# A hybrid decoder layer on one core: the sparse experts' second table summed on TensorE in four column strips, and token groups of 256, 384 and 384

## The chip, the core and the metric

One core of a Trainium2 chip runs the whole program; the other seven cores rest. The metric is the time of one execution on the device in microseconds (us), lower being better. The program was timed in three runs, and one further execution was profiled, from which all rows come.

## What is computed

One layer of a decoder, for 1024 prompt tokens of width 1024 and for 8 sample tokens with states of their own, all in float32. Three mixers read one combined input projection (88 blocks of 128 columns): a state-space scan (SSD), a convolution with 31 taps, and attention over 256 memory tokens. Their outputs are gated, merged, projected and normalised. Then each token picks 8 x 16 of 16,384 experts, and each expert is a row `u` of one table and a row `v` of another:

```python
def _peer_block(t, w_q, sub_keys, u_tab, v_tab):
    qv = (t @ w_q).reshape(nt, PEER_HEADS, 2, PEER_DHALF)
    s = jnp.einsum('thkd,hknd->thkn', qv, sub_keys)
    s_top, i_top = lax.top_k(s, PEER_TOPK)
    ...
    best, pos = lax.top_k(cand.reshape(nt, PEER_HEADS, PEER_TOPK * PEER_TOPK), PEER_TOPK)
    idx = jnp.take_along_axis(...)
    gate = jax.nn.softmax(best.astype(jnp.float32), axis=-1).astype(t.dtype)
    u = jnp.take(u_tab, idx, axis=0)
    act = jax.nn.gelu(jnp.einsum('td,thkd->thk', t, u), approximate=False)
    v = jnp.take(v_tab, idx, axis=0)
    return jnp.einsum('thk,thkd->td', gate * act, v)
```

The scan works in chunks of 128 tokens. Per chunk and head it needs the decays `exp(a_cs[l] - a_cs[s])` for l >= s, with `a_cs` a running sum over the chunk.

## The kernel before

**Groups.** The prompt passes in four groups (GROUPS 128, 128, 384, 384). For each, `front` loads the transposed tokens and computes the time steps (L465), and `main` runs the mixers over the group's input products (`proj`), its output products (`out_product`) and `merge`. A weight block is 128 x 1024. In the groups of 128 (PLAIN) a product is 8 matmuls in float32 (`product`, L197), each of which leaves two records. In the groups of 384, `load_w` splits a weight block in two fp32r parts (ScalarE L175, VectorE L177) and `mm3` multiplies three pairs of parts, 24 matmuls of one record each (L186). The output products are float32 matmuls (L197) everywhere. A product's result lies in one of three PSUM banks named mm. In `merge` a bank with an output product waits while another holds the product for its gate. The samples' columns ride with group 1 (RIDE).

**Decays.** For four heads of a chunk, `ssd_group` fills a bank with four mask matmuls in bf16 (L804) and four float32 matmuls that spread the running sums (L805), and ScalarE takes four exponentials.

**Routing.** When the next group begins, `routing` of the one before runs in small steps among its matmuls (`tick`): query products, top 16 on VectorE, and `route`. The last group's routing has no later group to run in.

**Sparse experts.** For the 640 tokens of the first three groups, `peer_block` and `peer_experts` treat 128 tokens at a time. For each of 128 slots GpSimd gathers 128 rows of the first table, one a token, into a buffer uv of 128 x 1024 (L404; five buffers), and VectorE multiplies each row by its token and sums it (L413). Then for each slot 128 rows of the second table are gathered, and VectorE adds them, scaled, to pacc (L423). The step of one slot is a row. `spread` puts rows between the products, PACE and PHASES rows a product; they are issued only after the fourth last of VectorE's other instructions (`issue_after` of `behind`), and at the lowest priority.

**Dense experts.** The last group's 384 tokens take all 16,384 experts (`dense_group`). First a table of gates is made in four steps: one-hot rows on VectorE (L1160), scalings on ScalarE (L1164), matmuls (L1165), and ScalarE's evictions (L1169). Meanwhile 30 of 128 blocks of activations (`x u`, L186 into the banks tp and sp) are computed and kept in memory. Then a loop over the 128 blocks loads and splits `v` (512 columns at a time), weighs the activations by the gates, and adds the second product into six banks (L1226). Rows of the sparse experts are spread through the loop, and what is left runs behind it.

The samples' attention (L990) already multiplies in strips: its four heads write 8 rows each at rows 0, 32, 64 and 96 of one bank, with stationary tiles of 8 columns.

A scheduler orders the instructions of each engine by priority and dependencies; each engine then works through its own queue in order. The numbers of lines below are those of the kernel before; a row of the changed kernel has the numbers of that kernel.

## Time and profile before

| what | us |
|---|---|
| median of three runs | 4664.98 |
| fastest and slowest run | 4653.48, 4665.51 |
| the profiled execution | 4662.57 |
| its span on the core | 4660.8 |
| TensorE matmuls busy | 4028.7 (86%) |
| VectorE busy | 3651.9 (78%) |
| GpSimd busy | 1822.1 (39%) |
| ScalarE busy | 1798.8 (39%) |

The DMA queues moved 1278.27 MB, 274 GB/s over the span. Busy time is the time in which an engine executes; the share is of the span. PE is TensorE's matmuls, PEld its weight loads (which overlap matmuls), DVE VectorE, ACT ScalarE, POOL GpSimd, SP the queue that issues plain transfers. The granted clock (PEclk) is a share of TensorE's full 2.4 GHz.

### The profile page before, as it was taken

What the parts mean: (1) busy time and instruction counts of PE and PEld (TensorE: products, weight loads), DVE (VectorE), ACT (ScalarE), POOL (GpSimd) and SP (SyncE); (2) the same over time, 40 slices, a digit from 0 to 9 for tenths busy, and PEclk for the clock granted to TensorE, in tenths of its full rate; (3) what the DMA queues carried; (4) which work ended last, traced back from release to release, by engine and by line L of the source; (5) the groups of instructions that cost most, each with busy time, mean ns of one, the idle gap of its engine ahead of it and who ended that gap; (6) DMA issues with size and microseconds to landing.
All of it is one profiled execution on the core that took longest, in us unless ns stands there. A gap on an engine that the chain in (4) does not pass through costs nothing.

```text
span 4660.8 us, 61736 instructions
## 1 busy us (share of the span) xinstructions
PE 4028.7 (86%) x20471; PEld 3289.6 (71%) x20471; DVE 3651.9 (78%) x7677; ACT 1798.8 (39%) x4112; POOL 1822.1 (39%) x1614
## 2 busy tenths in 40 slices
PE   9999966899878898899379898879887999789997
PEld 8999866787766665667267686645555788678886
DVE  1363478687888788778987899889785898788898
ACT  3434422274553312344136242022885333323334
POOL 0000034434424325534144544643012465556564
PEclk9999878898889999889688999999998999899999
DMA  6677678877657788867266976987568999899998
GB/s 198 208 238 232 202 296 315 339 247 275 207 184 275 278 286 317 317 227 244 106 236 225 325 249 231 371 279 265 182 218 290 341 387 368 250 356 354 364 386 304
DMA packets 436928, 1278.27 MB, mean 274 GB/s; under 512 B 45264, under 2 KB 119632, under 8 KB 434432
## 3 DMA queue, kind: packets, MB, share of 16 engines
q0 software_dynamic: 186880, 679.56, 41.2%
q1 hardware_dynamic: 249728, 594.77, 36.9%
q8 instruction: 161, 2.64, 0.2%
q14 instruction: 159, 1.30, 0.1%
HBM read 1220.22 MB, written 53.93 MB: 273 GB/s over the span
## 4 chain that ended last, share of the span: by engine, by line
issue 18%; DMA 15%; DVE 12%; PE 11%; POOL 8%; ACT 5%; POOLq 0%; SPq 0%; DVEq 0%; ACTq 0%
POOL uv L404 8%; DMA uv<-in_peer_v,idx 8%; DMA uv<-in_peer_u,idx 3%; PE mm L186 3%; DVE uv L413 2%; DVE pacc L423 2%; PE mm L197 2%; ACT xt L1169 2%; DVE b L535 2%; ACT e L1164 2%; DVE wl L177 1%; PE sp L186 1%; PE mm L1226 1%; DMA e<-in_peer_v 1%; DMA wr<-in_win 1%
## 5 line engine op out<-in xcount | busy, mean ns | idle before, releaser
L404 POOL DMA_INDIRECT uv<-in_peer_u,idx x640 | 800.9, 1251 | 1151.4 <-DVE uv L413 825.9
L404 POOL DMA_INDIRECT uv<-in_peer_v,idx x640 | 832.2, 1300 | 916.5 <-DVE pacc L423 571.9
L413 DVE SCALAR_TENSOR_TENSOR uv<-uv,x 128x1024 f32<-128x1024 f32 (+1 forms) x656 | 789.2, 1220 | 191.2 <-DMA uv<-in_peer_u,idx 173.5
L423 DVE SCALAR_TENSOR_TENSOR pacc<-uv,av,pacc 128x1024 f32<-128x1024 f32 (+1 forms) x650 | 833.0, 1282 | 103.7 <-DMA uv<-in_peer_v,idx 90.2
L186 PE MATMUL mm<-xt,wh 128*128 128x384 f32 x2816 | 793.2, 362 | 30.1 <-ACT wh L175 15.1
L197 PE MATMUL mm<-b,wr 128*128 128x128 f32 (+2 forms) x3072 | 747.8, 398 | 38.1 <-ACT b L648 14.4
L197 PEld LDWEIGHTS mm<-b,wr 128*128 128x128 f32 x3072 | 492.5, 201 | 241.0 <-issue 22.7
L175 ACT ACTIVATE wh<-wr 128x1024 fp32r<-128x1024 f32 x274 | 290.3, 1060 | 866.3 <-DMA wr<-in_win 330.9
L186 PEld LDWEIGHTS mm<-xt,wh 128*128 128x128 f32 x2816 | 541.0, 200 | 67.7 <-ACT wh L175 19.6
L186 PE MATMUL mm<-xt,wl 128*128 128x384 f32 x1408 | 505.3, 360 | 44.5 <-DVE wl L177 44.3
L535 DVE SCALAR_TENSOR_TENSOR b<-raw,cc,b 128x128 f32<-128x128 f32 (+1 forms) x960 | 444.6, 479 | 11.7 <-ACT b L533 4.7
L197 PE MATMUL mm<-xt,wr 128*128 128x128 f32 (+1 forms) x2816 | 368.5, 290 | 18.8 <-DMA wr<-in_win 8.9
L197 PEld LDWEIGHTS mm<-xt,wr 128*128 128x128 f32 x2816 | 354.3, 202 | 28.3 <-issue 11.9
L177 DVE TENSOR_TENSOR wl<-wr,wh 128x1024 fp32r<-128x1024 f32 x274 | 333.8, 1219 | 47.1 <-ACT wh L175 47.0
L186 PEld LDWEIGHTS mm<-xt,wl 128*128 128x128 f32 x1408 | 281.6, 200 | 61.1 <-DVE wl L177 53.5
L1226 PE MATMUL mm<-wh,b 128*128 128x512 f32 x768 | 246.4, 402 | 16.6 <-ACT b L150 16.6
L150 ACT ACTIVATE b<-acc 128x384 fp32r<-128x384 f32 x128 | 66.8, 525 | 377.0 <-PE st L1226 205.1
L186 PE MATMUL tp<-b,wh 128*128 128x384 f32 x784 | 206.9, 346 | 0.0
L186 PE MATMUL sp<-b,wh 128*128 128x384 f32 x784 | 203.5, 341 | 0.5 <-ACT b L682 0.5
L1165 PEld LDWEIGHTS mm<-e,e 128*128 128x128 f32 x768 | 119.4, 208 | 93.9 <-ACT e L1164 82.1
L1226 PE MATMUL ss<-wh,b 128*128 128x512 f32 x512 | 183.7, 399 | 0.0
L753 POOL COPY halo<-raw 128x3 f32<-128x3 f32 x96 | 51.0, 532 | 323.8 <-ACT raw L751 323.1
(392 smaller groups left out, 6951.3 us busy)
## 6 DMA issues: line engine op xcount, KB each, us to landing
wr<-in_win SPq DMA_DIRECT2D x352, 512.0 KB
wr<-in_peer_ut SPq DMA_DIRECT2D x128, 512.0 KB
e<-in_peer_v SPq DMA_DIRECT2D x256, 256.0 KB
wr<-in_wso SPq DMA_DIRECT2D x64, 512.0 KB
wr<-in_wq SPq DMA_DIRECT2D x64, 512.0 KB
gd<-xt SPq DMA_DIRECT2D x16, 1536.0 KB
xt<-gd SPq DMA_DIRECT2D x16, 1536.0 KB
wr<-in_wmo SPq DMA_DIRECT2D x32, 512.0 KB
```

Of the source, the lines that this page charges most:

```text
L175: act.activation(wh, wr, AF.Copy)
L177: dve.tensor_tensor(wl, wr, f32(wh), op=OP.subtract)
L186: pe.matmul(ps, a[:, k], b[k0 + k], start=(i == 0), stop=(i == n - 1))
L197: pe.matmul(ps, w[:, k], xs[k], start=(k == 0), stop=(k == 7))
L404: pool.indirect_dma_start(out=dst, out_offset=None, in_=table, in_offset=bass.IndirectOffsetOnAxis(ap=idx_col, axis=0))
L413: dve.scalar_tensor_tensor(u, u, 1.0, x1, op0=OP.mult, op1=OP.mult, accum_out=av[:, s:s + 1])
L423: dve.scalar_tensor_tensor(acc, v, av[:, s:s + 1], acc, op0=OP.mult, op1=OP.add)
L535: dve.scalar_tensor_tensor(cv, raw[:, i:i + nt], col(C_FW, j * TAPS + i), cv, op0=OP.mult, op1=OP.add)
L1164: act.activation(oj[:, u], oj[:, u], AF.Copy, scale=tr[:, 2, t + u:t + u + 1])
L1165: pe.matmul(pg[:, u * P:(u + 1) * P], oj[:, u], oi[:, u], start=True, stop=True)
L1169: act.activation(gs[:, :, o:o + TG].rearrange("p i t -> p t i"), pg.rearrange("p (t i) -> p t i", t=TG), AF.Copy)
L1226: pe.matmul(outs[2 * tbk + dh], a[:, ts], v[:, dh * 512:dh * 512 + 512], start=(c == 0 and i == 0), stop=(c == P - 1 and i == 2))
```

## The change

**Groups of 256, 384 and 384.** All products of input columns are split (no PLAIN group); the samples ride with group 0. A group's routing still runs in the next one.

**Sparse for 768 tokens, dense for 256.** The first 128 tokens of the last group become a sparse block too (SP); the dense part keeps the last 256 (DN), with 38 blocks of activations ahead of the loop instead of 30 (EARLY), and four banks for its sums instead of six.

**The second table on TensorE.** `block_u` works as before on the first table. It then transposes weights and indices, so that `block_v` can gather the 128 rows of one token into one buffer (a slot a partition). `four` multiplies it with a stationary tile of 32 columns of which one holds the token's weights, in two halves of 512 columns, into strip j (32 partitions) of the banks va. Token 32 j + m goes to strip j, so four tokens make a set. `four` is emitted VLAG, three rows, after the set's last gather. Streams for first table, second table and samples take turns (`row`).

**Decays.** The running sums are cut into three bf16 parts (cs3), and for four heads there is one mask matmul and one of 512 columns for the subtracted term, then four of 128 that add, and a single exponential over 512 columns.

**The rest.** Two mm banks instead of three, and sp becomes the bank st, which makes room for two va banks; eight uv buffers instead of five; halo copies on ScalarE instead of GpSimd; the sum of squares of the scan's output is collected in SBUF; a smaller area for DMA descriptors (4096).

```diff
-GROUPS = (128, 128, 384, 384)
+GROUPS = (256, 384, 384)
...
-QT = 24
+QT = 16
+SP = P
+DN = N - SP
...
-UVB = 5
-PLAIN = (0, 1)
-TICKS = (8, 5, 2, 3)
...
+UVB = 8
...
-PACE = (1.0, 2.0, 5.25)
...
+PACE = (3.0, 1.2, 2.4)
...
-RIDE = 1
+RIDE = 0
...
-EARLY = 30
-STEP = 4
+EARLY = 38
+STEP = 2
+VLAG = 3
+TLAG = 8
...
-        return psp.tile([P, 512], F32, name="mm", bufs=3)
+        return psp.tile([P, 512], F32, name="mm", bufs=2)
...
+    psm = pst
+    def pva():
+        return psp.tile([P, 512], F32, name="va", bufs=2)
...
+    slide = [cst.tile([P, 4, 63], F32, name=f"slide{i}") for i in range(2)]
+    for w in slide:
+        dve.memset(w, 0.0)
...
+    def row():
+        for _ in range(3):
+            i = turn[0] = (turn[0] + 1) % 3
+            queue, start = ((blocks, block_u), (weighed, block_v), (extra, iter))[i]
+            if streams[i] is None and queue:
+                streams[i] = start(queue.popleft())
+            if streams[i] is not None:
+                try:
+                    next(streams[i])
+                    return
+                except StopIteration:
+                    streams[i] = None
...
+            for x in late:
+                x[0] -= 1
+            while late and late[0][0] <= 0:
+                with tc.issue_after(lastpe):
+                    late.popleft()[1]()
             n = len(nc.cur_bb.bb.instructions)
             with tc.issue_after(last), tc.high_priority(-LATER):
-                try:
-                    next(experts[0])
-                except StopIteration:
-                    experts.popleft()
+                row()
...
+    def block_u(b):
+        g, c, idx, gate = b
+        x1 = pep.tile([P, D], F32, name="x1", bufs=1)
+        sp.dma_start(x1, x1d[g][c])
+        av = pep.tile([P, P], F32, name="av", bufs=2)
+        for s in range(P):
+            u = pep.tile([P, D], F32, name="uv", bufs=UVB)
+            gather(u, I["peer_u"], idx[:, c, s:s + 1])
+            dve.scalar_tensor_tensor(u, u, 1.0, x1, op0=OP.mult, op1=OP.mult, accum_out=av[:, s:s + 1])
+            yield
+        act.activation(av, av, AF.Gelu)
+        dve.tensor_tensor(av, av, gate[:, c], op=OP.mult)
+        def turned():
+            ix = blk(P)
+            act.activation(ix, idx[:, c], AF.Copy)
+            pt = pst()
+            pe.transpose(pt[:, 0:P], av, ident)
+            pe.transpose(pt[:, P:2 * P], ix, ident)
+            avt = pep.tile([P, P], F32, name="avt", bufs=2)
+            act.activation(avt, pt[:, 0:P], AF.Copy)
+            ixt = pep.tile([P, P], I32, name="ixt", bufs=2)
+            dve.tensor_copy(ixt, pt[:, P:2 * P])
+            weighed.append((g, c, avt, ixt))
+        late.append([TLAG, turned])
+    def block_v(b):
+        g, c, avt, ixt = b
+        va = []
+        def four(m, vs):
+            if m == 0:
+                va.extend(pva() for _ in range(2))
+            w = slide[m % 2]
+            act.activation(w[:, :, 31], avt[:, m:P:32], AF.Copy)
+            for dh in range(2):
+                for j in range(4):
+                    pe.matmul(va[dh][32 * j:32 * j + 32], w[:, j, 31 - m:63 - m], vs[j][:, dh * 512:dh * 512 + 512],
+                              start=(m == 0), stop=(m == 31))
+        for m in range(32):
+            vs = []
+            for j in range(4):
+                v = pep.tile([P, D], F32, name="uv", bufs=UVB)
+                gather(v, I["peer_v"], ixt[:, 32 * j + m:32 * j + m + 1])
+                vs.append(v)
+                if j < 3:
+                    yield
+            late.append([VLAG, lambda m=m, vs=vs: four(m, vs)])
+            yield
+        done = []
+        late.append([VLAG, lambda: done.append(1)])
+        while not done:
+            yield
+        xr = pep.tile([P, D], F32, name="uv", bufs=UVB)
+        sp.dma_start(xr, x1d[g][c])
+        for dh in range(2):
+            hs = slice(dh * 512, dh * 512 + 512)
+            dve.scalar_tensor_tensor(xr[:, hs], xr[:, hs], ALPHA, va[dh], op0=OP.mult, op1=OP.add)
+        layer_norm2(xr, P, pep.tile([P, D], F32, name="uv", bufs=UVB))
+        sp.dma_start(O[f"yp{g}"][c], xr)
...
+        pcs = pst()[:96, :tb * P]
+        da3 = blk(tb * 96)
+        dve.tensor_copy(da3.rearrange("p (c r h) -> p c r h", c=tb, r=3),
+                        da.unsqueeze(2).to_broadcast([P, tb, 3, 32]))
...
+            pe.matmul(pcs[:, c * P:(c + 1) * P], da3[:, c * 96:(c + 1) * 96], tri, start=True, stop=True)
+        cs3 = rp.tile([96, N], BF, name="cs3", bufs=1)[:, :nt]
+        act.activation(cs3, pcs, AF.Copy)
+        rest = blk(nt)[:96]
+        dve.tensor_tensor(rest, pcs, cs3, op=OP.subtract)
+        mid = blkp.tile([P, 2, N], BF, name="b")[64:96, 0, :nt]
+        act.activation(mid, rest[64:96], AF.Copy)
+        act.activation(cs3[32:64], rest[32:64], AF.Copy)
+        dve.tensor_tensor(cs3[64:96], rest[64:96], mid, op=OP.subtract)
+        G.cs3 = cs3.rearrange("p (c l) -> p c l", c=tb)
...
-            pool.tensor_copy(raw[:, 0:30], haloc[:, j])
-            pool.tensor_copy(haloc[:, j], raw[:, nt:nt + 30])
+            act.activation(raw[:, 0:30], haloc[:, j], AF.Copy)
+            act.activation(haloc[:, j], raw[:, nt:nt + 30], AF.Copy)
...
+                p = pst()[:, :nt]
                 for i in range(4):
-                    pe.matmul(ms, ones, sq[i], start=(q + i == 0), stop=(q + i == 6))
+                    pe.matmul(p, ones, sq[i], start=(i == 0), stop=(i == 3))
+                if q == 0:
+                    act.activation(ms, p, AF.Copy)
+                else:
+                    dve.tensor_tensor(ms, ms, p, op=OP.add)
...
+                j = 8 * q + 4 * i
+                pe.matmul(pg, identb, maskb.unsqueeze(1).to_broadcast([P, 4, P]), start=True, stop=False)
+                pe.matmul(pg, G.cs3[:, c], neg3[:, j:j + 4].unsqueeze(2).to_broadcast([96, 4, P]),
+                          start=False, stop=False)
                 for h in range(4):
-                    j = 8 * q + 4 * i + h
-                    pe.matmul(pg[:, h], identb, maskb, start=True, stop=False)
-                    pe.matmul(pg[:, h], ident[:32, j:j + 1].to_broadcast([32, P]), G.cst[:, c], start=False, stop=True)
-                for h in range(4):
-                    j = 8 * q + 4 * i + h
-                    act.activation(e4[:, h], pg[:, h], AF.Exp, bias=G.neg[:, c, j:j + 1])
+                    pe.matmul(pg[:, h], sel3[:, j + h:j + h + 1].to_broadcast([96, P]), G.cs3[:, c],
+                              start=False, stop=(h == 3))
+                act.activation(e4, pg, AF.Exp)
...
+        nb = SP // P if last else tb
+        G.idx = pep.tile([P, nb, P], I32, name=f"idx{g}")
         G.gate = pep.tile([P, tb, P], F32, name=f"gate{g}")
         G.top = sv, si
-        if not last:
-            route(P, tb, 8, sv, si, G.idx, G.gate)
-            experts.extend(peer_block(g, c, G.idx, G.gate) for c in range(tb))
+        route(P, nb, 8, *([x[:, 0:nb] for x in t] for t in G.top), G.idx, G.gate[:, 0:nb])
+        blocks.extend((g, c, G.idx, G.gate) for c in range(nb))
...
-        g, nt = G.g, G.nt
+        g, nt = G.g, DN
         nq = nt // QT
+        rs = [x[:, SP:] for x in G.rs]
...
-                for nm, nb in (("mm", 3), ("mm", 3), ("mm", 3), ("ss", 2), ("ss", 2), ("st", 1))]
+                for nm, nb in (("mm", 2), ("mm", 2), ("ss", 2), ("ss", 2))]
...
-    def peer_block(g, c, idx, gate):
-        x1 = pep.tile([P, D], F32, name="x1", bufs=1)
-        sp.dma_start(x1, x1d[g][c])
-        acc = pep.tile([P, D], F32, name="pacc")
-        yield from peer_experts(P, P, x1, idx[:, c], gate[:, c], acc)
-        xr = pep.tile([P, D], F32, name="uv", bufs=UVB)
-        sp.dma_start(xr, x1d[g][c])
-        dve.scalar_tensor_tensor(xr, xr, ALPHA, acc, op0=OP.mult, op1=OP.add)
-        layer_norm2(xr, P, acc)
-        sp.dma_start(O[f"yp{g}"][c], xr)
...
-    nc = bacc.Bacc("TRN2", target_bir_lowering=False, num_devices=1)
+    nc = bacc.Bacc("TRN2", target_bir_lowering=False, num_devices=1, dynamic_dma_scratch_size=4096)
```

What this does to the order of an engine's instructions, at three places. Rows are an engine's instructions in its own order: line, operation, result<-operands, shape.

**First place: TensorE, the last group's input and output products.** Before, this is the order there (mm is a bank for products, xt the tokens' two parts, wh and wl the two parts of a weight block, b a mixer's output block):

```order
L186 MATMUL mm<-xt,wh 128x384 x2
L186 MATMUL mm<-xt,wl 128x384
L197 MATMUL mm<-b,wr 128x392 x8
L186 MATMUL mm<-xt,wh 128x384 x2
L186 MATMUL mm<-xt,wl 128x384
L186 MATMUL mm<-xt,wh 128x384 x2
```

Now (L201 stands for L186, L212 for L197; names with their numbers):

```order
L488 MATMUL va_19340<-uv_20684,slide0_133 32x512
L488 MATMUL va_19341<-uv_20684,slide0_133 32x512
L201 MATMUL mm_20977<-xt_14372,wh_20999 128x384
L201 MATMUL mm_20977<-xt_14371,wl_21001 128x384
L212 MATMUL mm_21071<-b_20336,wr_21082 128x392
L212 MATMUL mm_21071<-b_20341,wr_21082 128x392
L212 MATMUL mm_21071<-b_20490,wr_21082 128x392
L212 MATMUL mm_21071<-b_20495,wr_21082 128x392
L212 MATMUL mm_21071<-b_20773,wr_21082 128x392
L488 MATMUL va_19340<-uv_20781,slide0_133 32x512
L488 MATMUL va_19341<-uv_20781,slide0_133 32x512
L212 MATMUL mm_21071<-b_20778,wr_21082 128x392
```

Between the matmuls of a product there now stand two matmuls of one token (both halves of its output, one stationary tile), and the next token's two come some matmuls later, so a set of four tokens does not stand together here. Of all 388 unbroken runs of L488, 306 are such pairs: 113 runs lie from the start of the second group to that of the last (302 matmuls), 189 in the last group (570), 18 among the gate tables (44), 66 in the dense loop, and 2 behind it (344 matmuls).

**Second place: TensorE, the dense loop.** Before, around the second product of a block (mm, ss and st are the banks of the sums, tp a bank for activations):

```order
L1226 MATMUL mm<-wh,b 128x512
L1226 MATMUL ss<-wh,b 128x512 x2
L1226 MATMUL st<-wh,b 128x512
L1226 MATMUL ss<-wl,b 128x512
L1226 MATMUL st<-wl,b 128x512
L1226 MATMUL ss<-wh,b 128x512
L1226 MATMUL st<-wh,b 128x512
L186 MATMUL tp<-b,wh 128x384 x2
L186 MATMUL tp<-b,wl 128x384
```

Now (L1345 stands for L1226):

```order
L1345 MATMUL mm<-wh,b 128x512 x2
L1345 MATMUL mm<-wl,b 128x512 x2
L1345 MATMUL mm<-wh,b 128x512 x2
L1345 MATMUL ss<-wh,b 128x512 x2
L1345 MATMUL ss<-wl,b 128x512 x2
L1345 MATMUL ss<-wh,b 128x512 x2
L488 MATMUL va<-uv,slide_133 32x512 x8
L201 MATMUL tp<-b,wh 128x256 x2
L201 MATMUL tp<-b,wl 128x256
```

The second product has 12 matmuls where it had 18, an activation's matmuls have 256 columns where they had 384, and a whole set of eight strip matmuls stands behind the second product. 59 of the 388 runs are whole sets like this one.

**Third place: VectorE, the last group's convolution.** Before (L535 is a tap, L423 a row of the second table, L590 and L591 `merge`, L177 a weight split):

```order
L423 SCALAR_TENSOR_TENSOR pacc<-uv,av,pacc 128x1024
L535 SCALAR_TENSOR_TENSOR b<-raw,cc,b 128x384
L590 TENSOR_TENSOR b<-b,mm 128x384
L535 SCALAR_TENSOR_TENSOR b<-raw,cc,b 128x384
L591 TENSOR_TENSOR acc<-acc,b 128x384
L535 SCALAR_TENSOR_TENSOR b<-raw,cc,b 128x384
L177 TENSOR_TENSOR wl<-wr,wh 128x1024
L535 SCALAR_TENSOR_TENSOR b<-raw,cc,b 128x384
L1054 TENSOR_TENSOR s_bc<-s_bc,proj_s 128x64
```

Now (L649 for L535, L455 a row of the first table, L709 and L710 for L590 and L591, L192 for L177):

```order
L649 SCALAR_TENSOR_TENSOR b<-raw,cc,b 128x384
L709 TENSOR_TENSOR b<-b,mm 128x384
L649 SCALAR_TENSOR_TENSOR b<-raw,cc,b 128x384
L710 TENSOR_TENSOR acc<-acc,b 128x384
L649 SCALAR_TENSOR_TENSOR b<-raw,cc,b 128x384
L192 TENSOR_TENSOR wl<-wr,wh 128x1024
L649 SCALAR_TENSOR_TENSOR b<-raw,cc,b 128x384
L455 SCALAR_TENSOR_TENSOR uv,av<-uv,x_18998 128x1024
L649 SCALAR_TENSOR_TENSOR b<-raw,cc,b 128x384
```

No row of the second table is left on VectorE; rows of the first stand among the taps instead. On GpSimd, 489 of the 1,568 gathers stand behind the first matmul of the dense second product, and 195 behind its last.

## Rows read from the trace of the kernel before

**Rows 1.** Six stretches: us, busy (instructions) of each engine, PEclk, DMA, GB/s

```profile
0.00:340.00 340.00, 321.91 (x2404) 301.40 (x2404) 137.19 (x445) 117.84 (x334) 14.42 (x71) 0.95 0.69 220
340.00:877.00 537.00, 430.03 (x3174) 401.60 (x3175) 321.02 (x1010) 178.25 (x570) 134.81 (x172) 0.88 0.78 273
877.00:1921.00 1044.00, 914.54 (x4439) 727.54 (x4437) 860.79 (x1826) 440.35 (x1035) 429.71 (x374) 0.90 0.76 264
1921.00:3258.00 1337.00, 1128.31 (x4696) 830.25 (x4696) 1160.13 (x2629) 440.14 (x1025) 611.92 (x521) 0.89 0.72 251
3258.00:3550.00 292.00, 234.85 (x1081) 164.02 (x1079) 213.31 (x503) 246.51 (x518) 32.90 (x30) 0.90 0.59 211
3550.00:4661.00 1111.00, 999.00 (x4684) 864.80 (x4684) 959.45 (x1267) 375.72 (x633) 598.36 (x447) 0.96 0.96 345
```

**Rows 2.** Groups by shape: busy us, mean ns, idle us before, releasers

```profile
L404 POOL DMA_INDIRECT uv<-in_peer_v,idx x640 | 832.2, 1300 | 916.5 <-DVE pacc L423 571.9 <-issue 65.2 <-DVE sb L921 50.7
L423 DVE SCALAR_TENSOR_TENSOR pacc<-uv,av,pacc 128x1024 f32<-128x1024 f32 x635 | 813.9, 1282 | 97.9 <-DMA uv<-in_peer_v,idx 90.2 <-issue 1.1
...
L413 DVE SCALAR_TENSOR_TENSOR uv<-uv,x 128x1024 f32<-128x1024 f32 x640 | 769.9, 1220 | 176.1 <-DMA uv<-in_peer_u,idx 173.5 <-issue 0.6 <-DVE uv L413 0.4
...
L177 DVE TENSOR_TENSOR wl<-wr,wh 128x1024 fp32r<-128x1024 f32 x274 | 333.8, 1219 | 47.1 <-ACT wh L175 47.0
```

**Rows 3.** Waits: engine, line, waited for: us in total, times, longest us

```profile
POOL uv L404 <- DVE uv L413: 890.1, 284, 51.4
POOL uv L404 <- DVE pacc L423: 613.2, 295, 83.0
...
DVE uv L413 <- DMA uv<-in_peer_u,idx: 173.5, 130, 4.5
...
POOL uv L404 <- issue: 139.2, 456, 0.7
...
DVE pacc L423 <- DMA uv<-in_peer_v,idx: 90.2, 106, 3.1
```

**Rows 4.** 20 us inside 1921 to 3258, columns as in rows 1

```profile
2240.00:2260.00 20.00, 0.00 (x0) 0.00 (x0) 20.00 (x107) 0.52 (x1) 0.00 (x0) 0.50 0.00 0
```

**Rows 5.** Timeline of TensorE around L990: start us, length us, instruction

```profile
1545.89 0.51 PE L186 MATMUL mm<-xt,wh 128*128 128x384 f32 x2
1546.34 1.05 PE L990 MATMUL sp<-wr,sb 128*8 128x256 f32 x16
1547.32 0.44 PE L186 MATMUL mm<-xt,wl 128*128 128x384 f32 x1
...
1572.94 0.60 PE L990 MATMUL sp<-wr,sb 128*8 128x256 f32 x2
```

**Rows 6.** L990: shortest, median, longest ns; first, last start

```profile
L990 PE MATMUL sp<-wr,sb x128: 379/379/631, 1546.3 to 1615.0; 128*8 128x256 f32 x128
```

**Rows 7.** Groups by shape again, columns as in rows 2

```profile
L197 PE MATMUL mm<-xt,wr 128*128 128x128 f32 x1408 | 181.3, 288 | 2.1 <-DMA wr<-in_win 2.0
...
L805 PE MATMUL ss<-cst,ident 32*128 32x128 f32 x512 | 151.6, 383 | 0.0
...
L1169 ACT ACTIVATE xt<-mm 128x512 f32<-128x512 f32 x96 | 138.4, 1442 | 7.7 <-PE mm L1165 7.1
...
L1164 ACT ACTIVATE e<-e,b 128x128 f32<-128x128 f32 x384 | 121.5, 391 | 4.5 <-DVE e L1160 4.5
...
L804 PE MATMUL ss<-maskb,identb 128*128 128x128 bf16 x256 | 63.5, 248 | 3.8 <-ACT bt L786 2.7 <-DVE hT L834 1.1
...
L197 PE MATMUL mm<-acc,wr 128*128 128x256 f32 x128 | 28.7, 387 | 0.0
```

**Rows 8.** L186 alone in two stretches: us, PE, PEld (records), PEclk, DMA

```profile
877.00:1921.00 1044.00, 436.19 (x2112) 388.65 (x2112) 0.90 0.76 264
...
3550.00:4661.00 1111.00, 452.04 (x2352) 424.29 (x2352) 0.96 0.96 345
```

**Rows 9.** L1226 alone in the last stretch, columns as in rows 8

```profile
3550.00:4661.00 1111.00, 573.47 (x2304) 438.72 (x2304) 0.96 0.96 345
```

115 lines of the change are left out of this document (57 added, 58 removed).

## Prediction

> **What bounds the kernel now.** The table of stretches comes first [rows 1]. Its cuts are where the next group's time-step matmuls (L465) or the next part of the dense experts (L1165, L1226) begin: A (0 to 877 us) holds the two groups of 128 tokens, B (877 to 1921) the first group of 384, C (1921 to 3258) the last group with its norm and routing, D (3258 to 3550) the gate tables, E (3550 to 4661) the dense loop and the end. The reader is to see TensorE busy for 322 + 430, 915, 1128, 235 and 999 us: it stands still for 125, 130, 209, 57 and 112 us, 633 in all. VectorE is 82% busy in B and 87% in C. The DMA engines are full in E alone, with a share of 0.96 at 345 GB/s. Next come the costliest groups [rows 2]: VectorE sums 635 rows of the second table at 1.28 us each, 814 us. Then the waits [rows 3]: gathers wait for VectorE to free a buffer (890 + 613 us), VectorE waits little for gathers (174 + 90). Last, one stretch of 20 us [rows 4]: VectorE routes without a pause and TensorE does nothing. This goes on from 2222 to 2300 us and is 78 of C's 209. So in A to C the bound is TensorE, at 84 to 88%, together with VectorE, and in E the transfers.
>
> **VectorE.** It loses 635 x 1.28 = 814 us. It gains 128 rows of the first table (768 instead of 640) at 1.22, 156 us, and 80 weight splits (354 instead of 274) at 1.22, 98 us [rows 2]. About 3,090 of 3,652 us stay, so it can no longer be the bound.
>
> **The second table on TensorE.** A gathered tile now holds the 128 rows of one token. Each needs two matmuls of 512 columns, one per half of the output, into one strip of 32 columns. The trace has this form with 256 columns, in the samples' attention (L990) [rows 5, 6]. A record lasts 0.38 us. Two records on one strip take 0.60, so the second starts 0.22 after the first. Sixteen records over four strips take 1.05: that is 0.38 and three more starts at 0.22, so the strips run four abreast. Each matmul leaves two records. The visit of sixteen also delays its neighbours: two of L186 start at 1545.89 and would be followed 0.35 later, but L990 starts at 1546.34, 0.10 late; L186 goes on at 1547.32, which is 0.98 later instead of 4 x 0.22, again 0.10.
> By this, a set of eight matmuls over four strips costs 4 x 0.43 + 0.19 = 1.91 us. A lone pair of one token has its four records on one strip, and costs 1.91 too. What it comes to is decided by the order: the 1,536 matmuls stand in 388 runs, of which 306 are lone pairs, as in the first place shown with the change, and only 59 whole sets, as in the second. At 1.91 a run, B has 113 (216 us), C 189 (361), D 18 (34) and E 66 before the dense matmuls end (126); two long runs behind them lie under gathers. That is 737 us, where 192 whole sets would be 367.
> The Trainium skill, TensorEngine Tiling (Array Packing), Theoretical Speedup, gives up to four times the speed for a dimension of 32 or less. The trace agrees for a whole set and not for a lone pair; by the page alone the second table would cost the 367, and the sum would be rival 2's.
>
> **A, one group of 256.** 88 input products took 2 x 16 records at 0.129 [rows 7], 4.13 us each. Now they are 24 matmuls of 264 columns in fp32r. No row has this form: it lies between the 0.129 and the 0.207 that 384 columns take (436.19 / 2112) [rows 8]. By columns from the latter it is 0.142, and 3.41 us: -63 (bounds -91 and +74). Forty output products of 256 columns at 0.224, for two of 128 each: -22 [rows 7]. The first routing moves to B: -33. Decays cost (151.6 + 63.5) / 64 = 3.36 us per four heads [rows 7]. They become six bf16 matmuls: four at 0.248, two with 384 columns more at 2.4 GHz, estimated 1.81 in all: -25 for 16 sets (bounds 0 and -54). Busy 752 - 143 = 609. Of the 125 idle most stood in the second group, beside gathers that are gone here; but now weights must be split, and two banks serve products instead of three: I take 55. **A = 664.**
>
> **B.** Busy 915, the routing of 256 tokens instead of 128 +24, 24 sets of decays -37: 902. TensorE will stand still less, so its granted clock (0.90 of full here, a mean over its levels of 1.2 and 2.4 GHz) should come near E's 0.96; at 0.95 the 902 are 855. Second table +216. Of 130 idle I keep two thirds, as VectorE is less full: 87. **B = 1158.**
>
> **C.** Busy 1128, decays -37, all three blocks' tokens copied out ahead of the dense part +10: 1101, and at 0.95 instead of 0.89, 1031. Second table +361. Idle: the 78 of routing stay, and two thirds of the other 131, 87. **C = 1557.**
>
> **D.** ScalarE is 84% busy with 96 evictions at 1.44 and 384 scalings at 0.39 [rows 7]. A third of both goes, 86 us. TensorE takes over as the bound: 235 - 46 of one-hot matmuls + 34 of the second table, 223, at the same 85%. **D = 260.**
>
> **E.** Now 345 GB/s x 1111 us = 383 MB, with 447 gathers of 0.524 MB [rows 1]. After the change it is 489 gathers (256 MB), 90 tiles of the first table (47), 128 of the second (67), gates (17) and kept activations (4): 391 MB, 1133 us at the same rate. TensorE's part of the loop is 2,160 matmuls of 256 columns at two thirds of 0.192 [rows 8], 277 us; 1,536 of 512 at 0.249 [rows 9], 382; and 126: 785 us against 838 of transfers, close enough that I add 15. 195 gathers stand behind the last dense matmul. There GpSimd issues one in 1.30 + 0.31 us [rows 2, 3], 314 us, 18 more than the transfers. **E = 1166.**
>
> **At no price:** the halo copies on ScalarE (39% busy); eight gather buffers for five, of which four wait for a set; the smaller descriptor area; the sums of squares in SBUF. GpSimd's cover is its idle time; where it fails, gathers are late, and that is rival 3.
>
> **Sum:** 664 + 1158 + 1557 + 260 + 1166 = 4805, and 2 around the span: 4807 against the profiled 4662.6. The median of the runs is 4665.0, so I add 2 and forecast 4810.
>
> **Rivals.**
> 1. *TensorE's waits go with VectorE's load (faster).* Place: A to C. For it: VectorE is the busiest beside TensorE there, and loses 560 us. Against: the few waits for VectorE that the table names are gathers', and the routing stretch stays whole. Price: idle falls to 20 in A, 26 in B, 78 + 26 in C, D to 245, and E's 15 go: 629 + 1097 + 1496 + 245 + 1151 + 4 = 4622. It decides from 160 us less idle than the 307 that I keep. Chance 0.25.
> 2. *Four abreast everywhere.* For it: L990's runs [rows 5]. Against: other matmuls stand between the pairs in the order. Price: the 916 matmuls of B, C and D as 115 sets are 219 us instead of 611: 4810 - 392 = 4418. Chance 0.08.
> 3. *TensorE waits for gathers and banks (slower still).* Its queue goes in order: a pair waits for its gather, and behind it every product, then that product's eviction and the next weight buffers wait. With two banks, each of 24 merges in a group holds one until VectorE has read it, an estimated 2.5 us after the gate product (ScalarE's sigmoid, two VectorE operations and what stands before them): 180 us over three groups. Price 4990. Against: a pair's gather can go out four tokens ahead. Chance 0.19.
> 4. *No change.* Rival 1 in part, 4651 to 4679. Chance 0.06.
>
> **Chances.** The forecast has 0.42, with 4690 to 4930 of its own. A measurement of this kernel can't tell 0.3% (14 us) from no change. Faster: 0.25 + 0.08 = 0.33; same 0.06; slower 0.42 + 0.19 = 0.61. The range for 8 in 10 leaves out rival 2 and what lies past rival 3: 4460 to 5020. The bounds of the 264 columns (-28, +137) and of the decays over three groups (+99, -116) lie inside it.
>
> **What would show it.** Right: L488 with one start each 0.43 us in B and C and some 700 us before the tail; VectorE near 3,090; C over 1,500 us with TensorE at 88% or more; a DMA share of 0.95 in the dense loop; a last stretch near 300 us in which only gathers run. Wrong: L488 under 400 us (rival 2); TensorE idle for less than 150 us in A to C (rival 1); TensorE waiting over 150 us for uv tiles or for evictions of mm (rival 3); 264 columns at over 0.17 us a start; a DMA rate over 370 GB/s at the end.

## The result, and the profile after

The changed kernel takes 4984.0 us (four runs, 4980.2 to 4987.5) against 4664.2: a ratio of 1.069, interval 1.067 to 1.071. The direction was forecast, the size was not: +145 us were predicted, +320 came.

The table of stretches of the kernel after, cut at the same places (columns as in [rows 1]; only C's end is a little earlier, where the gate tables' first transposes begin, 7 us ahead of their first matmuls, and the part behind the last dense matmul stands in a line of its own):

```profile
0.00:622.00 622.00, 563.07 (x3680) 512.00 (x3680) 333.85 (x648) 294.07 (x727) 0.20 (x4) 0.98 0.44 144
622.00:1977.00 1355.00, 1135.48 (x4978) 744.36 (x4974) 873.60 (x2145) 465.84 (x1102) 492.50 (x415) 0.91 0.73 252
1977.00:3601.00 1624.00, 1443.72 (x5810) 853.17 (x5810) 1055.98 (x2772) 473.21 (x1136) 676.13 (x607) 0.94 0.76 262
3601.00:3847.00 246.00, 198.74 (x949) 140.84 (x947) 160.02 (x337) 148.87 (x365) 75.00 (x63) 0.91 0.78 261
3847.00:4652.00 805.00, 768.73 (x4255) 573.18 (x4258) 535.46 (x901) 324.13 (x608) 321.57 (x289) 0.98 0.98 355
4652.00:4981.00 329.00, 260.70 (x694) 60.78 (x686) 61.84 (x87) 32.69 (x79) 189.93 (x195) 0.92 0.90 335
```

The five parts against the forecast: A 622 (664), B 1355 (1158), C 1624 (1557), D 246 (260), E 805 + 329 = 1134 (1166). B alone missed by 197 us. Subtract the first two columns and TensorE stands still for 220 us in B (87 were kept) and 180 in C (165). VectorE's 3021 us are the predicted 3,090 within 3%.

The same stretches, the strip matmuls (L488) alone, TensorE's columns only:

```profile
622.00:1977.00 1355.00, 237.62 (x604) 44.64 (x604) 0.91 0.73 252
1977.00:3601.00 1624.00, 368.08 (x1140) 70.99 (x1140) 0.94 0.76 262
3601.00:3847.00 246.00, 43.06 (x88) 7.73 (x88) 0.91 0.78 261
3847.00:4652.00 805.00, 129.96 (x557) 25.63 (x560) 0.98 0.98 355
```

Ahead of the tail that is 238 + 368 + 43 + 130 = 779 us; 737 were predicted. What a lone pair costs is seen in the timeline of TensorE in the last group (start, length, instruction):

```profile
2978.12 1.90 PE L488 MATMUL va<-uv,slide 128*32 128x512 f32 x4
2979.96 0.44 PE L201 MATMUL mm<-xt,wh 128*128 128x384 f32 x1
2980.24 0.34 PE L201 MATMUL mm<-xt,wl 128*128 128x384 f32 x1
2980.51 1.90 PE L488 MATMUL va<-uv,slide 128*32 128x512 f32 x4
2982.34 0.62 PE L201 MATMUL mm<-xt,wh 128*128 128x384 f32 x2
```

One token's two matmuls, four records, take 1.90 us, and the next product starts 1.84 us after their start. All four write one strip. No wait stands between: the products before and behind run on. That is close to the forecast's price of 1.91, which was to hold the neighbours' delay as well. With it, a pair costs 0.10 + 1.83 + 0.11 = 2.04 us: the second pair starts 0.27 us after the product's matmul before it, and the matmul behind the first pair is followed 0.28 later, where 0.17 is usual.

Of the costliest groups by shape (columns as in [rows 2]) these answer to [rows 2, 7]: the strip matmuls, the gate tables' evictions, and the three kinds of matmul of the decays.

```profile
L488 PE MATMUL va<-uv,slide 128*32 128x512 f32 x3072 | 1035.4, 615 | 127.8 <-DMA uv<-in_peer_v,ixt 118.5 <-issue 7.7 <-ACT slide L485 1.3
...
L1290 ACT ACTIVATE xt<-mm 128x512 f32<-128x512 f32 x64 | 66.6, 1053 | 16.3 <-PE mm L1286 16.1
...
L925 PE MATMUL ss<-cs,sel 96*128 96x128 bf16 x256 | 27.1, 224 | 0.0
L921 PE MATMUL ss<-maskb,identb 128*128 128x512 bf16 x64 | 25.8, 402 | 3.0 <-ACT bt L904 1.9 <-DVE hT L953 1.1
...
L922 PE MATMUL ss<-neg,cs 96*128 96x512 bf16 x64 | 25.3, 396 | 0.0
```

And the split products alone (L201), in A and B, which answer to [rows 8]:

```profile
0.00:622.00 622.00, 287.62 (x2112) 269.28 (x2112) 0.98 0.44 144
622.00:1977.00 1355.00, 427.52 (x2112) 373.72 (x2112) 0.91 0.73 252
```

And the waits that answer to [rows 3]:

```profile
POOL uv L443 <- PE va L488: 941.5, 347, 20.0
...
POOL uv L443 <- DVE uv L455: 794.3, 189, 74.4
...
PE va L488 <- DMA uv<-in_peer_v,ixt: 118.5, 61, 7.5
...
PE mm L212 <- ACT b L708: 39.0, 27, 4.4
```

The gathers still wait for buffers, only now it is TensorE that frees most of them. TensorE itself waits little for gathers, 118.5 us in all. The last row is `merge`: an output product waits for a bank until the sigmoid of a gate (L708) has been taken.

### The profile page after: what moved, and what is told of

Same layout as the page of the kernel before. It is cut to its first block, busy times and chain, and to the rows that moved or that the text cites. A ratio compares the mean times of both kernels' runs of the same rounds, so it can differ in the third digit from the quotient of the medians.

```text
span 4980.9 us, 59884 instructions
## 1 busy us (share of the span) xinstructions
PE 4370.4 (88%) x20352; PEld 2884.3 (58%) x20352; DVE 3020.7 (61%) x6885; ACT 1738.8 (35%) x4017; POOL 1755.3 (35%) x1572
## 5 line engine op out<-in xcount | busy, mean ns | idle before, releaser
L443 POOL DMA_INDIRECT uv<-in_peer_v,ixt x768 | 805.8, 1049 | 1055.6 <-PE va L488 589.5
L488 PE MATMUL va<-uv,slide 128*32 128x512 f32 x3072 | 1035.4, 615 | 127.8 <-DMA uv<-in_peer_v,ixt 118.5
L201 PE MATMUL mm<-xt,wh 128*128 128x384 f32 (+1 forms) x4224 | 1054.3, 334 | 51.9 <-ACT b L891 28.7
L455 DVE SCALAR_TENSOR_TENSOR uv<-uv,x 128x1024 f32<-128x1024 f32 x768 | 920.7, 1218 | 172.8 <-DMA uv<-in_peer_u,idx 121.3
L201 PEld LDWEIGHTS mm<-xt,wh 128*128 128x128 f32 x4224 | 741.8, 192 | 164.7 <-issue 85.3
L212 PE MATMUL mm<-b,wr 128*128 128x256 f32 (+2 forms) x2304 | 738.8, 468 | 61.9 <-ACT b L708 32.2
L192 DVE TENSOR_TENSOR wl<-wr,wh 128x1024 fp32r<-128x1024 f32 x354 | 432.3, 1222 | 486.8 <-ACT wh L190 405.4
L201 PE MATMUL mm<-xt,wl 128*128 128x384 f32 (+1 forms) x2112 | 692.6, 328 | 39.0 <-DVE wl L192 38.5
L488 PEld LDWEIGHTS va<-uv,slide 128*32 128x32 f32 x3072 | 209.4, 111 | 740.2 <-issue 544.3
L212 PEld LDWEIGHTS mm<-b,wr 128*128 128x128 f32 x2304 | 430.9, 194 | 344.8 <-issue 87.6
L201 PEld LDWEIGHTS mm<-xt,wl 128*128 128x128 f32 x2112 | 405.3, 192 | 76.6 <-DVE wl L192 44.1
L649 DVE SCALAR_TENSOR_TENSOR b<-raw,cc,b 128x384 f32<-128x384 f32 (+1 forms) x720 | 408.4, 568 | 14.6 <-ACT b L647 6.2
L177 DVE TENSOR_TENSOR wl<-e,wh 128x512 fp32r<-128x512 f32 x256 | 165.6, 687 | 61.2 <-ACT wh L165 47.0
L1345 PE MATMUL mm<-wh,b 128*128 128x512 f32 x512 | 165.4, 402 | 11.8 <-ACT b L165 11.7
L1345 PE MATMUL ss<-wh,b 128*128 128x512 f32 x512 | 165.1, 403 | 0.0
L212 PE MATMUL mm<-acc,wr 128*128 128x256 f32 (+2 forms) x512 | 150.5, 445 | 6.8 <-ACT b L708 6.8
```

The source lines that it names most:

```text
L177: dve.tensor_tensor(l, src, f32(h), op=OP.subtract)
L192: dve.tensor_tensor(wl, wr, f32(wh), op=OP.subtract)
L201: pe.matmul(ps, a[:, k], b[k0 + k], start=(i == 0), stop=(i == n - 1))
L212: pe.matmul(ps, w[:, k], xs[k], start=(k == 0), stop=(k == 7))
L443: pool.indirect_dma_start(out=dst, out_offset=None, in_=table, in_offset=bass.IndirectOffsetOnAxis(ap=idx_col, axis=0))
L455: dve.scalar_tensor_tensor(u, u, 1.0, x1, op0=OP.mult, op1=OP.mult, accum_out=av[:, s:s + 1])
```

## The experiments

Each ratio is to the kernel before, measured in the same session. "Behind" is the number of gathers that stand behind the last dense matmul, with the time from there to the end. "A to C" is the time to the gate tables' first transposes. The number 9 is not used.

| kernel | ratio | interval | A to C, us | behind |
|---|---|---|---|---|
| before | 1 | | 3249 | 0 |
| changed | 1.069 | 1.067–1.071 | 3601 | 195, 329 us |
| 1 whole sets | 1.035 | 1.033–1.037 | 3412 | 195, 383 us |
| 2 table on VectorE | 1.032 | 1.027–1.036 | 3077 | 537, 830 us |
| 3 sums in another bank | 1.094 | 1.092–1.096 | 3696 | 195, 324 us |
| 4 before + decays | 0.974 | 0.971–0.976 | 3105 | 0 |
| 5 table on VectorE, dense 384 | 0.980 | 0.977–0.982 | 3041 | 56, 123 us |
| 6 whole sets, tables in turn | 1.012 | 1.009–1.014 | 3329 | 203, 384 us |
| 7 whole sets, sums in another bank | 1.039 | 1.036–1.042 | 3393 | 195, 390 us |
| 8 before + decays + banks | 1.000 | 0.998–1.001 | 3242 | 0 |
| 10 as 5, three mm banks | 0.970 | 0.966–0.974 | 2943 | 105, 186 us |
| 11 as 6, transposes later | 1.006 | 1.004–1.008 | 3338 | 203, 378 us |
| 12 as 10, more rows | 0.972 | 0.969–0.975 | 2991 | 91, 168 us |
| 13 as 10, sums in another bank | 0.975 | 0.973–0.977 | 2879 | 144, 266 us |

### 1. Are the broken pairs the cost?

```diff
-            for dh in range(2):
-                for j in range(4):
-                    pe.matmul(va[dh][32 * j:32 * j + 32], w[:, j, 31 - m:63 - m], vs[j][:, dh * 512:dh * 512 + 512],
-                              start=(m == 0), stop=(m == 31))
+            with tc.high_priority(1000):
+                strip(3, 0)
+                head = nc.cur_bb.bb.instructions[-1]
+                with tc.issue_after(head):
+                    for j, dh in ((0, 0), (1, 0), (2, 0), (3, 1), (0, 1), (1, 1), (2, 1)):
+                        strip(j, dh)
```

(`strip(j, dh)` is the matmul of the removed lines.)

> The changed kernel with the eight strip matmuls of a set tied together: the strip that waits for the last gather goes first, the other seven are issued right behind it. 150 unbroken runs stand where 388 were: 36 for 113 in the second group, 72 for 189 in the last, 5 for 18 among the gate tables, 35 for 66 in the dense loop. Theory (a run costs about 2 us whatever its strips, as records of one strip can't overlap and those of four can): L488 falls by some 160 us in B, 230 in C and 30 in D, and the time to about 4570 (4540 to 4660, the upper end if whole sets wait longer for their last gather). Rival one (a matmul costs the same in a pair as in a set): 4984 as before. Rival two (a set that waits for its last gather holds up TensorE's queue as long as it saves): 4800 to 4984, with TensorE waiting over 150 us more for uv tiles.

4821 us: 3.4% of the kernel before came back, 163 us where 414 were expected. The strip matmuls alone in B, C and the dense loop:

```profile
621.00:1896.00 1275.00, 93.73 (x592) 18.25 (x592) 0.88 0.74 265
1896.00:3412.00 1516.00, 169.20 (x1152) 33.80 (x1152) 0.90 0.78 283
...
3652.00:4442.00 790.00, 72.51 (x564) 15.26 (x568) 0.97 0.99 363
```

238 became 94, 368 became 169, 130 became 73: the price did fall as the theory says, by 343 us in B and C. But the two stretches became only 80 and 108 us shorter, and the end 54 longer. TensorE's idle time in B and C grew by 145 us. The largest part of that are the waits for the second table's tiles, which rose from 118.5 us to this:

```profile
PE va L487 <- DMA uv<-in_peer_v,ixt: 416.4, 112, 16.8
```

Of it 147 us lie in B and C, where it was 43, and 223 behind the dense loop. Rival two took the larger half of the gain. The timeline of two sets (16 records each) in the dense loop shows what a whole set costs:

```profile
3731.35 3.64 PE L487 MATMUL va<-uv,slide 128*32 128x512 f32 x16 [3.11 <-DMA uv<-in_peer_v,ixt]
...
3752.59 1.92 PE L487 MATMUL va<-uv,slide 128*32 128x512 f32 x16
```

Without a wait it takes 1.92 us, as long as a lone pair, which does a quarter of the work. Behind a wait of 3.11 it takes 3.64. The same two spans as stretches (columns as in [rows 1]) show why: the granted clock was 0.50 in the slow one and 1.00 in the fast one.

```profile
3731.35:3734.99 3.64, 3.64 (x17) 0.67 (x17) 1.59 (x4) 0.00 (x0) 2.09 (x2) 0.50 0.86 271
3752.59:3754.51 1.92, 1.92 (x18) 0.48 (x17) 0.97 (x2) 0.32 (x1) 0.00 (x0) 1.00 1.14 319
```

Of the 147 sets of this kernel ahead of the end, 104 ran wholly at 1.00 and took 1.92 us, 31 of them behind a wait of their own; the 14 that ran wholly at 0.50 took 3.64; the others lie between. In B and C together TensorE worked 346 us at 0.50, against 215 in the changed kernel. So kernel 1 gave back its gain in two ways, as idle time and as a lower clock for more of its work.

### 2. The second table back on VectorE

```diff
-UVB = 8
+UVB = 7
...
+        acc = pep.tile([P, D], F32, name="pacc")
+        for s in range(P):
+            v = pep.tile([P, D], F32, name="uv", bufs=UVB)
+            gather(v, I["peer_v"], idx[:, c, s:s + 1])
+            if s == 0:
+                dve.tensor_scalar(acc, v, av[:, 0:1], None, op0=OP.mult)
+            else:
+                dve.scalar_tensor_tensor(acc, v, av[:, s:s + 1], acc, op0=OP.mult, op1=OP.add)
+            yield
```

(`turned`, `block_v` and `four` are left out of this kernel.)

> The changed kernel with the second table back on VectorE (scaled and added row by row, seven uv buffers and one sum buffer), all else as in the change: groups of 256, 384 and 384, dense experts for 256 tokens, decays in bf16 parts. Theory (the strip matmuls are what the change costs): TensorE loses the 606 us of L488 in B and C, but VectorE gains 193 us of rows in B and 365 in C and becomes as full there, so B about 1180, C about 1480, and the whole 4660 (4580 to 4760). Rival (the regrouping itself costs the time, by routing two and three blocks at once and by the banks): 4850 or more.

4803, between theory and rival. A to C are as short as the theory has them (3077 us), but the end (columns as in [rows 1]) shows where the time went:

```profile
3980.00:4810.00 830.00, 4.07 (x6) 0.19 (x4) 706.76 (x829) 31.61 (x48) 604.16 (x537) 0.50 0.94 348
```

TensorE works 4 us of the last 830, in which GpSimd issues 537 gathers. VectorE, 79% busy in B and 93% in C, frees the gathers' buffers later: 757 gathers were issued in B and C, against 1,021 in the changed kernel.

### 3. The normaliser's sums in another bank

```diff
-                p = pst()[:, :nt]
+                p = ptp()[:, :nt]
```

> The changed kernel with the sum of squares taken in the bank tp instead of st, which the samples' state products share since the change. Theory (the 80 us in which TensorE stands still between 1178 and 1285 us come from the normaliser's sums queueing for st behind the samples): 4905 (4880 to 4950). Rival (the samples' own chain holds up TensorE's queue, whichever bank the sums use): 4984 within 20.

5087, slower still. The stall near 1200 us went (TensorE's waits for the samples' state products in B fell from 54 to 8 us) and B's idle from 220 to 187, but the order moved: C has 274 runs of strip matmuls where it had 189. Their row in C:

```profile
1966.00:3696.00 1730.00, 533.37 (x1252) 100.74 (x1252) 0.95 0.74 255
```

533 / 274 = 1.95 us a run, and 368 / 189 = 1.95 in the changed kernel: 85 runs more, 165 us more, with only a tenth more matmuls (626 for 570). So this run missed its own question and answered the first: a run has a price, a matmul in it hardly any.

### 4. The decays alone

The kernel before with `cs3`, `neg3`, `sel3` and the single exponential, as in the change's diff, and nothing else of it.

> The kernel before with the decays from bf16 parts and nothing else of the change. Theory (the prediction's term: 3.36 us per four heads become 1.81, 64 times, on an engine that is the bound there): 99 us less TensorE work, and a time of 4566 to 4605. Rival (TensorE's saved time turns into waits for VectorE, which is 82 to 87% busy): 4640 to 4665.

4528, faster than the theory's range. Its A and B:

```profile
0.00:823.00 823.00, 698.27 (x5484) 662.64 (x5484) 458.98 (x1463) 285.06 (x854) 150.04 (x243) 0.94 0.78 270
823.00:1824.00 1001.00, 845.40 (x4291) 675.34 (x4290) 854.22 (x1824) 427.04 (x963) 431.10 (x369) 0.92 0.77 273
```

In A and B TensorE's busy time falls by 54 and 69 us against [rows 1], and the stretches by 54 and 43: as TensorE gets less to do they get shorter, and in B a part of it turns into idle time. It is faster than the theory's range, as a set got cheaper than the 1.81 us booked (1.22 in the changed kernel) and the clock came up too: TensorE's work at a granted clock of 0.50 fell from 115 to 52 us in A and from 161 to 92 in B.

### 5 to 7. Dense experts back to 384; buffers; the bank again

5 is kernel 2 with `SP = 0`, `QT = 24`, the paces of the kernel before in the dense part (`PACE`, `EARLY`, `STEP`), and banks mm, ss and va for the six sums. 6 is kernel 1 with `VLAG = 4` and

```diff
-            i = turn[0] = (turn[0] + 1) % 3
+        for i in (1, 2, 0):
```

in `row`. 7 is kernel 1 with 3's edit.

> The kernel of the second experiment (second table on VectorE) with the dense experts back at 384 tokens (30 blocks ahead of the loop, paces of the kernel before, six banks for the sums), so that of the change the groups of 256, 384, 384, the decays and the banks remain. Theory (in the second experiment the 256 gathers that the moved 128 tokens bring stand at the end, 1.55 us each, while the groups cost nothing): A to C as there, 3077 us, and the dense part and the end as in the kernel before, 1411 us, with some 60 gathers more behind it, 93 us: 4580 (4540 to 4640). Rival (the regrouping itself costs the time): 4700 or more.

> The kernel of the first experiment (whole sets) with the streams not alternating: all rows of a block's first table, then all of its second, and a set multiplied four rows after its last gather instead of three. Then the eight uv buffers hold two sets instead of one set and four rows of the first table, so that a set's gathers can land while the set before is multiplied. Theory (whole sets gave back half of their gain because TensorE waits 416 us for uv tiles, as alternate rows leave no buffer for the next set): those waits fall to about half, and the time from 4821 to about 4670 (4600 to 4740). Rival (a set waits for the transfer itself, not for buffers): 4821 within 40.

> The kernel of the first experiment (whole sets) with the sums of squares in the bank tp instead of st. In the third experiment the stall of B went but 85 more broken pairs in C hid it; whole sets can't break. Theory (st, shared with the samples' state products, stalls TensorE for some 70 us near 1190 to 1270 us): 4750 (4720 to 4790). Rival (the stall is the samples' own chain, or moves elsewhere): 4821 within 20.

5 gave 4562, the theory's 4580: regrouping did not slow A to C, and the 128 tokens moved from dense to sparse, with the paces that go with them, cost 5.2% with the table on VectorE (1.032 - 0.980). 6 gave 4706, also the theory's: with room for two sets, TensorE's waits for the second table fall from 416 to 177 us, but those for the weights (av) appear:

```profile
PE st L464 <- DVE av L457: 217.0, 5, 133.7
PE va L486 <- DMA uv<-in_peer_v,ixt: 176.5, 66, 12.5
```

So at the same groups the second table in whole sets, one table after the other, beats VectorE by 2.0% (1.012 against 1.032 in kernel 2): what made it lose are the broken sets and the alternating streams.

7 gave 4832, the rival's: C is 43 us shorter than in 1, B 24 longer, the dense loop and the end 19 longer. The stall did go (TensorE's waits near 1200 us for the samples' state products fell from 67 to 5 us), but TensorE's waits for the second table's tiles in B rose from 67 to 123.

### 8. The banks alone

The kernel of experiment 4 with two mm banks, sp merged into st, the sums of squares in SBUF, 27 work tiles instead of 28, and va banks for two of the dense sums.

> The kernel of the fourth experiment (before, with the new decays) with two mm banks instead of three, the samples' bank sp merged into st, the sums of squares in SBUF, and 27 instead of 28 work tiles to make room for them. Prediction's rival three (with two banks each merge holds one until VectorE has read it: 180 us over three groups): 4700 or more. Theory (banks are a small part of the change, a stall of the samples near 70 us at most): 4530 to 4600.

4655, in the middle. The banks take back the whole 2.6% that the decays gave: A grows from 823 to 876 us, B from 1001 to 1081. Of B's 80 us, 38 are busy time: TensorE's work at a granted clock of 0.50 is up from 92 to 161 us.

### 10 to 13. What would beat both

10 is kernel 5 with three mm banks and one va; 11 is kernel 6 with `TLAG = 24`; 12 is kernel 10 with 4.2 and 4.8 rows a product; 13 is kernel 10 with 3's edit.

> The kernel of the fifth experiment (groups of 256, 384, 384, second table on VectorE, dense experts for 384 tokens) with three mm banks; the bank va that its samples then don't need is the third. Theory (in the eighth experiment two banks and a shared st cost 126 us, of which the waits of products for evictions in merge are the part that the third bank gives back): 4562 falls to 4480 (4440 to 4520), below every kernel so far. Rival (the 126 us came from the samples' sharing of st, which stays here): 4562 within 20.

> The kernel of the sixth experiment (whole sets, the tables in turn) with the weights' transposes emitted 24 rows after a block's last row of the first table instead of 8. There TensorE waits 217 us for them, in five places, 134 us the longest, since they stand in its queue ahead of the rows that they need. Theory (a later place costs nothing and frees the products behind it): the waits for av fall below 60 us and the time from 4706 to about 4600 (4560 to 4660). Rival (most of the 217 us lies at the end, where nothing else is to do, and only 45 us lie in C): 4660 to 4710.

> The kernel of the tenth experiment (table on VectorE, dense 384, three banks) with 4.2 and 4.8 rows a product in the second and last group instead of 3.5 and 4. It leaves 105 gathers for the end, 186 us. Theory (VectorE has 20% left in B, so most of them fit ahead of the dense part): the end falls below 90 us and A to C grow by less than 60: 4460 (4420 to 4510). Rival (VectorE is the bound in B and C, and rows that are asked for earlier only push its other work back): 4500 to 4560.

> The kernel of the tenth experiment with the sums of squares in the bank tp, as in the third and seventh. There too TensorE stands still near 1164 to 1231 us, where the sums of squares (L624) stand behind three steps of the samples' state products (L991) for the bank st, two gaps of 28 us. Theory (the stall is the shared bank's and costs its whole length where no strip matmuls wait behind it): 4517 falls to 4450 (4430 to 4480). Rival (as in the seventh experiment the time comes back as other waits in the same stretch): 4517 within 20.

10 gave 4517, at the slow end of its theory and the fastest of all, 3.0% below the kernel before; the third bank is worth 1.0%, so it is a part of the 2.6%. TensorE's waits for the sigmoid in `merge`, 52.5 us in kernel 5, are gone with it. In 11 and 12 the rivals held (4691 and 4531).

13 gave 4540, no faster than 10 (the intervals of the ratios overlap), though its reason was right. The stall in kernel 10 (L991 are the samples' state products, L624 the sums):

```profile
1196.88 2.08 PE L991 MATMUL st<-ident,proj_s 128*128 128x128 f32 x8 [28.27 <-ACT sb L994]
...
1230.61 2.08 PE L991 MATMUL st<-ident,proj_s 128*128 128x128 f32 x8 [28.84 <-ACT sb L994]
1233.43 5.19 PE L624 MATMUL st<-b,ones 128*128 128x384 f32 x8 [0.74 <-ACT sb L994]
```

B and the end of kernel 10, and then of kernel 13:

```profile
592.00:1699.00 1107.00, 898.71 (x4360) 713.33 (x4360) 890.88 (x2036) 452.64 (x1054) 352.64 (x274) 0.88 0.69 239
...
4337.00:4523.00 186.00, 3.00 (x5) 0.19 (x4) 165.10 (x133) 22.53 (x35) 110.37 (x105) 0.51 0.90 344
```

```profile
587.00:1638.00 1051.00, 896.23 (x4365) 710.70 (x4362) 839.36 (x1982) 448.73 (x1048) 297.46 (x237) 0.91 0.66 231
...
4270.00:4536.00 266.00, 3.44 (x7) 0.37 (x5) 213.58 (x197) 23.80 (x37) 176.00 (x144) 0.51 0.88 318
```

The stall went and B lost 56 us. But in B 37 gathers fewer were issued, and behind the dense part 39 more: the end grew by 80 us. While TensorE stood still, rows had been done that now come last.

## Why the prediction was wrong, by its own steps

**Right.** The price of a run (1.91 predicted; 1.90 for a pair and 1.92 for a set measured at the full clock, 2.04 with the neighbours' delay) and from it the second table's 737 us (779). The Trainium skill's TensorEngine Tiling (Array Packing), Key Properties, has different tiles work in parallel and a change of the tiling mode drain the engine. The traces agree with the first for a set; a pair stays on one tile, so this gives it nothing. The drain can't be told apart within the 1.84 us of a pair. D, E and VectorE's load were within 6%, and of the signs that were to show the forecast right the strip matmuls' time, VectorE's load, TensorE's 89% in C, the DMA share of 0.98 in the dense loop and the last stretch of 329 us came (though TensorE was busy for 261 of it). No sign was set for B's length, where most of the miss lay. Rival 2's price of whole sets holds, but kernel 1 shows that more than half of what it saves returns as waits.

**The miss in parts.** Against the forecast's five parts 176 us are too many: 88 of TensorE's work in B and C (first step below), 133 of idle time in B (second step) and 15 in C, 29 of strip matmuls in B and C, less 42 in A, 14 in D and 32 in E (177 as rounded). That the last three came under was luck for the sum.

**Mis-sized, first step: "at 0.95 the 902 are 855" in B, and 1101 to 1031 in C.** 117 us were taken off because TensorE's granted clock would rise from 0.90 and 0.89 to 0.95. Measured without the strips, TensorE works 1135 - 238 = 898 us in B and 1444 - 368 = 1076 in C: 29 us less than 902 and 1101, where 117 were booked. That mean mixes working and idle time, so the stretches at 0.50, the level of 1.2 GHz, have to be looked at, and whether TensorE worked in them. In one of B's before, it never stood still (columns as in [rows 1]):

```profile
927.71:934.54 6.83, 6.83 (x26) 6.17 (x27) 2.39 (x8) 2.21 (x10) 0.00 (x0) 0.50 0.28 95
```

In B before, a matmul of 384 columns (L186) follows the one before it after 0.17 us at full clock and after 0.32 at 0.50. Summed over all stretches at 0.50, with each engine's busy time in them: B and C before, then B and C after.

```profile
sum 214.99, PE 160.88 PEld 130.12 DVE 178.01 ACT 94.70 POOL 59.91; mean PE 5.96 PEld 4.82 DVE 6.59 ACT 3.51 POOL 2.22
sum 300.36, PE 175.36 PEld 132.60 DVE 263.98 ACT 92.33 POOL 97.11; mean PE 6.49 PEld 4.91 DVE 9.78 ACT 3.42 POOL 3.60
...
sum 252.56, PE 125.01 PEld 77.77 DVE 196.57 ACT 85.29 POOL 95.46; mean PE 6.25 PEld 3.89 DVE 9.83 ACT 4.26 POOL 4.77
sum 198.00, PE 89.69 PEld 55.42 DVE 166.49 ACT 52.33 POOL 83.64; mean PE 6.90 PEld 4.26 DVE 12.81 ACT 4.03 POOL 6.43
```

TensorE worked at 0.50 for 161 + 175 = 336 us before and 125 + 90 = 215 after. The direction was right, then, and the size was not: of 121 us less at 0.50 a little under half is won (0.32 to 0.17), an estimated 56 of the 117. In B the mean hardly rose (0.90 to 0.91): 128 us of idle time at 0.50 stand there now, where 54 did. Another 42 us are the neighbours' share of 302 runs (2.04 - 1.90 each, as in the timeline above), which the forecast's 1.91 did not cover. Against that the decays gave 28 us more than booked (48 sets at 1.22 us, below, instead of 1.81). That makes 75 of the 88; the rest is open.

**Mis-sized, second step: "Of 130 idle I keep two thirds", 87 us in B.** It was 220: it rose by 90 where it was to fall by 43. Two of TensorE's waits in B, after:

```profile
PE va L488 <- DMA uv<-in_peer_v,ixt: 35.8, 15, 6.5
PE mm L201 <- DVE wl L192: 29.7, 5, 27.9
```

and of the samples' state products before, in its B:

```profile
PE sp L909 <- ACT sb L912: 21.2, 5, 18.1
```

The largest piece is the samples' state, which now comes after their attention and shares st with the sums of squares (these stood under "at no price"). The timeline of TensorE there:

```profile
1205.41 2.08 PE L1028 MATMUL st<-ident,proj_s 128*128 128x128 f32 x8 [13.58 <-ACT sb L1031]
1208.23 2.08 PE L1028 MATMUL st<-ident,proj_s 128*128 128x128 f32 x8 [0.73 <-ACT sb L1031]
1240.18 2.08 PE L1028 MATMUL st<-ident,proj_s 128*128 128x128 f32 x8 [29.87 <-ACT sb L1031]
1251.01 0.47 PE L465 MATMUL st<-ident,av 128*128 128x128 f32 x1 [8.76 <-DVE av L458]
...
1259.04 2.07 PE L1028 MATMUL st<-ident,proj_s 128*128 128x128 f32 x8 [7.34 <-DVE ixt L470]
```

Five gaps add up to 60 us, where the samples' state waited 21 before, and what stands behind these rows in TensorE's queue waits with them. Two of the five, 16 us, are the transposes of the second table's weights (L465), which use st too. The other three are not the second table's: kernel 5, without strips, has the same stall (L991 waits 82 us for ScalarE there). That the shared bank makes it is shown by kernels 3, 7 and 13, where it goes as soon as the sums have another bank. Another 28 us are one wait for a weight split (L192) behind VectorE's routing, now of 256 tokens; all waits for splits are 30 us where they were 21. With the 36 us of waits for the second table's tiles, these account for 39 + 9 + 36 = 84 of the 90. VectorE's lower load shortened none of these.

**Smaller, the other way.** A came 42 us under: a decay set takes (25.8 + 25.3 + 27.1) / 64 = 1.22 us, not 1.81, and a matmul of 264 columns 287.6 / 2112 = 0.136, not 0.142. These two are 22 of the 42; for A the forecast booked nothing for the clock, and there it rose most, from 0.95 and 0.88 to 0.98. D came 14 under; an eviction fell from 1.44 to 1.05 us. E came 32 under.

**The rivals.** Rival 3's time (4990) was met, but that is a coincidence. TensorE waits 118.5 us for gathers in the whole kernel, and 79 in B to D and the dense loop. `merge`, priced at 180 us from an estimate of 2.5 a merge that no run shows, waits 39.0 us in 27 places. Either is under the 150 that were to be its sign. Its banks are real all the same: experiment 8 has 2.6% for them, and the largest piece of B's new idle time hangs on the shared bank st, which the prediction gave no price. Rival 1's mechanism failed: B and C have 400 us of idle where there were 338, with VectorE 65% busy.

**Where the 320 us come from,** one step at a time, as shares of the kernel before: decays -2.6% (experiment 4); banks +2.6 (8); groups, splits, halo copies and the rest that goes with them -2.0 (5); 128 tokens from dense to sparse +5.2 (2); the second table on TensorE in whole sets +0.4 (1); the sets broken into pairs +3.4 (the change). The sum is 6.9 before rounding. Each step is measured on top of the ones before it and would differ in another order; the fifth also brings the alternating streams, which cost 2.4% of their own (6 against 1), and the second is several edits in one, of which only the third mm bank was tried by itself (10).

**Open.** What B's stall costs in the changed kernel: in three kernels (3, 7, 13) it was removed and the whole got no faster, as other waits or the end grew. Which part of the third step gives the 2.0%. The last 13 of the 88 us in the first step.

## What to carry to other kernels

Matmuls that run side by side on different strips do so only if they stand side by side in the queue: count the runs in the order, and price the run, not the matmul. A mean clock over a stretch does not say whether the engine worked or stood still at the lower level; sum the stretches at that level, with the busy time in them, before you book a faster clock. And where a backlog is worked off at the end, a stall removed ahead of it may buy nothing, for the work that it hid comes back last: look at what is left behind the last dense matmul as well as at the stretch that you shortened.
